# Gate and up projection of a decoder layer: eight k tiles instead of four in one Strassen group, in pieces of 2048 columns

## The chip, the cores and the metric

The kernel runs on one core of one Trainium2 chip. Its time is the device time of one execution in microseconds. Engines: PE is the matrix engine (TensorE), DVE VectorE, ACT ScalarE, POOL GpSimd, SP SyncE, which only issues transfers. 128 partitions of on-chip memory (SBUF) hold the operands; matmuls write into PSUM banks of 128x512 fp32.

## The reference

One layer over 256 tokens of width 2048, in fp32. The changed parts:

```python
def rms_norm(x, g):
    return x * rsqrt(mean(x * x, axis=-1) + EPS) * g

x = x + mixer(rms_norm(x, mix_g))        # pooling and gated delta rule, reads h @ w_in first
x = x + cross_attention(rms_norm(x, xa_g), mem)
h = rms_norm(x, ffn_g)
g = causal_conv3(h @ w_gate) ; u = h @ w_up          # 2048 -> 5632 each
x = x + (silu(g) * u) @ w_down                       # 5632 -> 2048
return rms_norm(x, final_norm_g)
```

(The names of the gains are shortened.) Gate, up and down are the larger part of the arithmetic.

## The kernel before

**Arithmetic.** Every fp32 operand is split into a high part (a cast to the matmul's 32-bit format, on ACT) and a low part (operand minus high part, on DVE). A product is three matmuls: high by high, high by low, low by high (in `product`, lines L876 to L878; 128 rows of weights by 512 columns each). The function `parts` splits a piece of weights: L940 on ACT, L941 on DVE, into tiles `wh` and `wl`.

**Gate and up.** The 5632 columns are handled in 11 blocks (`for b in range(NB)`), each of 512 gate and 512 up columns. A token tile is 128 tokens, and there are two; the sum over 2048 runs over 16 tiles of 128 ("k tiles"). Take a 2x2 product: two halves of tokens, two halves of k, and as column halves gate and up. The weights are b11 (gate, first k half), b12 (up, first half), b21 and b22. For a group of four k tiles (`JS = (0,)`) this product is done by Strassen's scheme in Winograd's form: seven products instead of eight, on sums of the weights (t1 = b11+b12, t2 = t1+b22, t3 = b12+b22, later t2+b21, lines L965 to L969 and L1004 on DVE) and sums of the activations (S3, S5, S6, S7, made once, in `hS`). The other twelve k tiles (`JP`) are done plainly, eight products each group of four. A product there is six matmuls. Banks b1, b2, b3, b5, b6, b7 collect the products; q1 (a copy of b1, L977 on ACT), u2, q1 and c22 (L978 to L980) combine them, and L996 to L1007 scale them by the tokens' factor r3 into c11, c12, c21, c22, L1006 (c11) once a block.

**Rest of a block.** c11 to c22 are turned by 16 transposes (L907), convolved, put through Silu and multiplied into `af` (`convolve`). These steps run in the next block as a "job", a generator that `pump` advances after products. Most blocks' `af` are stored to HBM (`aspill`) and loaded again for the down projection (`arow`).

**Loads.** SP issues all weight loads in program order, each waiting for a free buffer: `wr` has 6 of 0.5 MB, `wh` and `wl` 5 each. The order of the instructions on each engine comes from a scheduler that places the program's operations; the lists below print it.

**Down** uses the same `parts` and buffers, pieces of 0.5 MB. At its end come the residual `fin`, its squares, the final norm with its gain (POOL, L1077) and the stores, t = 0 and then t = 1.

**Start.** x comes in transposed (`xraw`), is scaled and split (L104 on ACT, L105 on DVE, into `hT`), and multiplied by small weights `ba` (bank bps) and by w_in (in_k, weights w0 and then wi, columns in stretches of 128 called h here: h0, h1, h2, ...). The squares for the first norm, xss and xsq, run on POOL (L242 to L245); xsum (L280, DVE) sums them, and a chain xsum, rxps, rx, rxpb brings the norm's factor to PE.

Of the kernel before, what the change touches and what calls it, by code (L numbers as in the profile page):

```python
# [41 lines left out]
def hybrid_trunk(ctx, tc, a, out):  # L42
# [154 lines left out]
    with tc.tile_pool(name="dn", bufs=1, reuse_waits="tile") as dn:  # L197
# [71 lines left out]
        def decays():  # L269
# [9 lines left out]
            with tc.issue_after(last_split[0].ins):  # L279
                dve.tensor_reduce(xsum, xss.rearrange("p k t -> p t k"), AX.X, ALU.add)  # L280
# [591 lines left out]
    def product(ps, stat, j, w, first=False, last=False):  # L872
        for i in range(2):
            xh, xl = stat(j, i)
# [3 lines left out]
            m = pe.matmul(ps, xl, wh, start=False, stop=last and i == 1, skip_group_check=True)  # L878
        pump(m)
# [50 lines left out]
    raw = lambda b, j, w: fp.tile([P, 2, 512], F32, name="wr", tag="wr", bufs=6)  # L930

    def load(b, j, w):
        r = raw(b, j, w)
        nc.sync.dma_start(r, a["w_gu"][b, j, :, w])
        return r

    def parts(src):
# [6 lines left out]
    slot = [0]

    def sumtile():
        slot[0] += 1
        return ring[:, slot[0] % 8].rearrange("p (i c) -> p i c", i=2)

    def results():  # L950
        return [fp.tile([P, 512], F32, name=n, tag=n, bufs=1) for n in ("c11", "c12", "c21", "c22", "q1", "u2")]

    job("xr", rows_of_x())
    c11, c12, c21, c22, q1, u2 = results()
    JS, JP = (0,), (1, 2, 3)
    for b in range(NB):
        b1, b3, b5, b6, b7 = (bank(n) for n in ("b1", "b3", "b5", "b6", "b7"))
        t2s, b21s = {}, {}
        for j in JS:
# [6 lines left out]
            product(b5, S5, j, parts(t1), first=f_, last=l_)
            dve.tensor_tensor(t2, t1, b22, ALU.add)
            product(b6, S6, j, parts(t2), first=f_, last=l_)
            dve.tensor_tensor(t3, b12, b22, ALU.add)  # L969
            product(b7, S7, j, parts(t3), first=f_)  # L970
            t2s[j] = t2
            b21s[j] = load(b, j, 3)
# [192 lines left out]
```

## Time and profile before

| | |
|---|---|
| median of 3 runs | 1547.29 us (1545.36 to 1548.23) |
| the profiled execution | 1547.02 us |
| its span, first to last instruction | 1545.2 us |
| busy: PE, DVE, ACT, POOL | 1499.6, 1068.6, 825.7, 205.7 us |
| moved by DMA | 290.83 MB, 188 GB/s in the mean |

A row of a timeline has a start, a duration, the engine, the line of the kernel, the operation with its output and input, and in brackets how long the engine stood idle before it and what released it. An operation's row is longer than the pitch at which a pipelined engine starts the next: rows overlap.

### The profile page before, as it was taken

How to read it: one execution, taken by the hardware profiler on the slowest of the kernel's cores; microseconds unless marked ns; L12 is line 12 of the kernel's file. 1: busy time of each engine (PE TensorE's matmuls, PEld its weight loads, DVE VectorE, ACT ScalarE, POOL GpSimd, SP SyncE). 2: the span in 40 equal slices, each digit the busy share in tenths (PEclk: the TensorE clock that was granted, in tenths of full speed). 3: DMA queues.
4: the chain of work that ended last, by engine and by line, in shares of the span. 5: the costliest groups of instructions: out<-in, count | busy, mean ns of one | idle time of the engine just before them, and what ended most of it. 6: DMA issues, size and time to landing. Idle time of an engine off the chain costs nothing.

```text
span 1545.2 us, 20429 instructions
## 1 busy us (share of the span) xinstructions
PE 1499.6 (97%) x7788; PEld 1271.9 (82%) x7788; DVE 1068.6 (69%) x1400; ACT 825.7 (53%) x1210; POOL 205.7 (13%) x210
## 2 busy tenths in 40 slices
PE   5999999999999999999979999999999999999997
PEld 3788789888888888998868888888888888888885
DVE  7978887676544676666757778877787886555444
ACT  3555766554444554555546666555556665444433
POOL 4342533341100121001220000000000000000002
PEclk9999999999999999999989999999999999999999
DMA  5445443447555555444538666666666678655562
GB/s 197 169 162 175 174 153 134 139 177 266 192 179 192 185 188 187 146 150 158 188 117 259 206 209 193 193 194 211 215 206 204 202 243 316 199 194 191 194 193 77
DMA packets 67378, 290.83 MB, mean 188 GB/s; under 512 B 11344, under 2 KB 11728, under 8 KB 51152
## 3 DMA queue, kind: packets, MB, share of 16 engines
q1 hardware_dynamic: 66992, 289.01, 54.8%
q8 instruction: 61, 1.00, 0.3%
q10 hardware_dynamic: 288, 0.52, 0.1%
q14 instruction: 37, 0.30, 0.1%
HBM read 279.93 MB, written 9.57 MB: 187 GB/s over the span
## 4 chain that ended last, share of the span: by engine, by line
PE 87%; DVE 7%; POOL 2%; DMA 1%; ACT 1%; issue 1%; SPq 1%; DVEq 0%; POOLq 0%; ACTq 0%
PE b L877 10%; PE b L878 10%; PE b L876 10%; PE acc L1041 5%; PE acc L1043 5%; PE acc L1042 5%; PE xq L142 4%; PE xo L142 4%; PE mix L142 4%; PE kk L142 3%; PE pvs L695 2%; PE pvs L694 2%; PE pvs L693 2%; PE xq L143 2%; PE xo L143 2%; PE mix L143 2%
## 5 line engine op out<-in xcount | busy, mean ns | idle before, releaser
L940 ACT CAST wh<-wr 128x1024 fp32r<-128x1024 f32 x165 | 172.6, 1054 | 141.1 <-PE b L878 134.1
L876 PE MATMUL b<-wh,hP 128*128 128x512 f32 x594 | 233.2, 393 | 6.3 <-ACT wh L940 6.3
L941 DVE TENSOR_TENSOR wl<-wr,wh 128x1024 fp32r<-128x1024 f32 x165 | 199.1, 1220 | 51.1 <-ACT wh L940 50.8
L877 PE MATMUL b<-wl,hP 128*128 128x512 f32 x594 | 231.9, 390 | 0.7 <-DVE wl L941 0.7
L878 PE MATMUL b<-wh,hP 128*128 128x512 f32 x594 | 231.7, 390 | 0.0
L941 DVE TENSOR_TENSOR wl<-wd,wh 128x1024 fp32r<-128x1024 f32 x88 | 107.6, 1224 | 103.8 <-ACT wh L940 103.8
L940 ACT CAST wh<-wd 128x1024 fp32r<-128x1024 f32 x88 | 92.6, 1056 | 120.6 <-PE acc L1043 114.3
L876 PEld LDWEIGHTS b<-wh,hP 128*128 128x128 f32 x594 | 111.7, 188 | 29.2 <-ACT wh L940 6.6
L877 PEld LDWEIGHTS b<-wl,hP 128*128 128x128 f32 x594 | 111.8, 188 | 23.8 <-DVE wl L941 1.2
L878 PEld LDWEIGHTS b<-wh,hP 128*128 128x128 f32 x594 | 111.8, 188 | 23.3
L1041 PE MATMUL acc<-wh,aring 128*128 128x512 f32 x320 | 124.5, 389 | 0.0
L1042 PE MATMUL acc<-wl,aring 128*128 128x512 f32 x320 | 124.5, 389 | 0.0
L1043 PE MATMUL acc<-wh,aring 128*128 128x512 f32 x320 | 124.5, 389 | 0.0
L101 DVE TENSOR_TENSOR wil<-wi,wih 128x1024 fp32r<-128x1024 f32 x78 | 100.5, 1293 | 11.9 <-ACT wih L100 11.5
L1077 POOL TENSOR_TENSOR fin<-fin 128x512 f32<-128x512 f32 x6 | 7.7, 1284 | 720.0 <-ACT fj L1075 719.8
L100 ACT CAST wih<-wi 128x1024 fp32r<-128x1024 f32 x78 | 81.4, 1049 | 8.0 <-DMA wi<-in_w_in 3.3
L142 PE MATMUL xq<-h2T,wqh 128*128 128x512 f32 x240 | 84.9, 393 | 0.0
L142 PE MATMUL kk<-mT,wkh 128*128 128x512 f32 x240 | 84.4, 393 | 0.0
L142 PE MATMUL xo<-oT,woh 128*128 128x512 f32 x240 | 84.3, 392 | 0.0
L142 PE MATMUL mix<-yT,wmh 128*128 128x512 f32 x240 | 84.1, 392 | 0.0
L101 DVE TENSOR_TENSOR wvl<-wv,wvh 128x1024 fp32r<-128x1024 f32 x32 | 39.7, 1240 | 45.3 <-ACT wvh L100 45.3
L1042 PEld LDWEIGHTS acc<-wl,aring 128*128 128x128 f32 x320 | 60.1, 188 | 12.6
(466 smaller groups left out, 3634.3 us busy)
## 6 DMA issues: line engine op xcount, KB each, us to landing
wr<-in_w_gu SPq DMA_DIRECT2D x176, 512.0 KB, 5.0
wd<-in_w_down SPq DMA_DIRECT2D x88, 512.0 KB, 4.7
wi<-in_w_in SPq DMA_DIRECT2D x39, 1024.0 KB, 4.9
wk<-in_w_k SPq DMA_DIRECT2D x16, 1024.0 KB, 4.9
wv<-in_w_v SPq DMA_DIRECT2D x16, 1024.0 KB, 4.9
wm<-in_w_mix SPq DMA_DIRECT2D x16, 1024.0 KB, 4.9
wq<-in_w_xq SPq DMA_DIRECT2D x16, 1024.0 KB, 4.9
wo<-in_w_xo SPq DMA_DIRECT2D x16, 1024.0 KB, 4.9
```

The costliest lines, as they stand in the source:

```text
L100: act.copy(hi, src)
L101: return dve.tensor_tensor(lo, src, hi.bitcast(F32), ALU.subtract)
L142: pe.matmul(ps, h, full, start=kk == 0, stop=False)
L143: i = pe.matmul(ps[:, T:], l, xt[:, 0, :], start=False, stop=False)
L876: pe.matmul(ps, xh, wh, start=first and i == 0, stop=False, skip_group_check=True)
L877: pe.matmul(ps, xh, wl, start=False, stop=False, skip_group_check=True)
L878: m = pe.matmul(ps, xl, wh, start=False, stop=last and i == 1, skip_group_check=True)
L940: act.copy(h, src)
L941: dve.tensor_tensor(l, src, h.bitcast(F32), ALU.subtract)
L1041: pe.matmul(acc[t, n], ah, wh, start=first, stop=False)
L1042: pe.matmul(acc[t, n], ah, wl, start=False, stop=False)
L1043: return pe.matmul(acc[t, n], al, wh, start=False, stop=last)
```

## The change

The k tiles fall into two groups of eight, q = 0 in the Strassen form and q = 1 plain. A product is twelve matmuls, a piece of weights 128x2048 (1 MB). `wr` has 4 buffers, `wh` and `wl` 3 each. b11 is loaded into `tt`, a part of `ring` (two halves, by b % 2), and grows there: b11, plus b12, plus b22, plus b21. The first and third of these sums are transfers from HBM that add to what lies in SBUF, issued by POOL (`join`); the second, and b12 + b22 (in place), are DVE's. So b12 and b21 are read twice. c11 to c22 and `af` move into other parts of `ring`. In the host's layout the weights are cut accordingly.

At the start the squares of x move from POOL to ACT (four of 128x1024), and xsum reduces all 16 tiles at once. In down the pieces are 1 MB, `fin` is loaded late among the weights, and at the end the gain is multiplied on DVE, t = 0's scaling falls into t = 1's sums, and the four stores are 512 KB.

```diff
-            xc = xraw[c // 2][:, (c % 2) * 4:(c % 2) * 4 + 4]
-            if c == 0:
-                pool.tensor_tensor(xss, xc, xc, ALU.mult)
-            else:
-                pool.tensor_tensor(xsq[:, c * 4:c * 4 + 4], xc, xc, ALU.mult)
-                pool.tensor_tensor(xss, xss, xsq[:, c * 4:c * 4 + 4], ALU.add)
+        for c in range(4):
+            act.activation(xsq[:, c * 4:c * 4 + 4], xraw[c // 2][:, (c % 2) * 4:(c % 2) * 4 + 4], AF.Square)
...
-                dve.tensor_reduce(xsum, xss.rearrange("p k t -> p t k"), AX.X, ALU.add)
+                dve.tensor_reduce(xsum, xsq.rearrange("p k t -> p t k"), AX.X, ALU.add)
...
-    def product(ps, stat, j, w, first=False, last=False):
-        for i in range(2):
+    def product(ps, stat, q, w, first=False, last=False):
+        for i in range(4):
...
+    def join(t, b, w):
+        nc.gpsimd.dma_start(t, a["w_gu"][b, 0, :, w], accum_op=ALU.add)
+
+    results = lambda: [ring[:, 4 + n // 2, (n % 2) * 512:(n % 2 + 1) * 512] for n in range(4)]
...
-        for j in JS:
-            f_, l_ = j == JS[0], j == JS[-1]
-            b11, b22, b12 = load(b, j, 0), load(b, j, 2), load(b, j, 1)
-            product(b1, A11, j, parts(b11), first=f_)
-            product(b3, S3, j, parts(b22), first=f_)
-            t1, t2, t3 = sumtile(), sumtile(), sumtile()
-            dve.tensor_tensor(t1, b11, b12, ALU.add)
...
+        tt = ring[:, 2 * (b % 2):2 * (b % 2) + 2].rearrange("p j (i c) -> p (j i) c", i=2)
+        nc.sync.dma_start(tt, a["w_gu"][b, 0, :, 0])
+        b22, b12 = load(b, 0, 2), load(b, 0, 1)
+        product(b1, A11, 0, parts(tt), first=True)
+        join(tt, b, 1)
+        product(b3, S3, 0, parts(b22), first=True)
+        dve.tensor_tensor(b12, b12, b22, ALU.add)
+        product(b7, S7, 0, parts(b12), first=True)
...
+        w = parts(load(b, 1, 1))
+        product(b3, A11, 1, w)
+        product(b2, A21, 1, w, first=True)
+        product(b5, S5, 0, parts(tt), first=True, last=True)
+        dve.tensor_tensor(tt, tt, b22, ALU.add)
+        w = parts(load(b, 1, 2))
+        product(b3, A12, 1, w, last=True)
+        product(b2, A22, 1, w, last=True)
+        product(b6, S6, 0, parts(tt), first=True, last=True)
+        join(tt, b, 3)
...
-        for j in JP:
...
+        w = parts(load(b, 1, 0))
+        product(b1, A11, 1, w)
+        product(b7, A21, 1, w)
+        w = parts(load(b, 1, 3))
+        product(b1, A12, 1, w)
+        product(b7, A22, 1, w)
...
+        product(b1, A12, 0, parts(load(b, 0, 3)), last=True)
+        product(b7, A22, 0, parts(tt), last=True)
...
-    fin = big("fin", [P, 3, D], F32)
-    for t in range(2):
-        nc.sync.dma_start(fin[:, t], xspill[t])
-    nc.sync.dma_start(fin[:, 2], a["fin_row"])
...
+            if m == NB - 2:
+                fin = big("fin", [P, 3, D], F32)
+                for t in range(2):
+                    nc.sync.dma_start(fin[:, t], xspill[t])
+                nc.sync.dma_start(fin[:, 2], a["fin_row"])
+        w = rows(k, 0, 4)
...
-            if n < 3:
-                pool.tensor_tensor(fin[:, t, c], fin[:, t, c], fin[:, 2, c], ALU.mult)
...
+            if (t, n) != (1, 3):
+                with tc.issue_after(i.ins):
+                    dve.tensor_tensor(fin[:, t, c], fin[:, t, c], fin[:, 2, c], ALU.mult)
```

In the changed kernel the split's lines are L938 (ACT) and L939 (DVE), the sums L957 (b12) and L966 (tt), the joins L943, u2, q1 and c22 L974 to L976, the scaling of c11 L990, the squares L249 and xsum L275.

SP's queue from the last xo weights into gate/up, before:

```order
L109 DMA wo<-in_w_xo 128x2048 x16
L934 DMA wr<-in_w_gu 128x1024 x7
L893 DMA xspill<-xt 128x512
L934 DMA wr<-in_w_gu 128x1024 x3
L893 DMA xspill<-xt 128x512
L934 DMA wr<-in_w_gu 128x1024
```
After the loads of w_xo came those of `wr`, with the stores of x between them. The same place now (`ring` is tt):

```order
L109 DMA wo<-in_w_xo 128x2048 x16
L952 DMA ring<-in_w_gu 128x2048 x2
L933 DMA wr<-in_w_gu 128x2048 x3
L891 DMA xspill<-xt 128x512
L933 DMA wr<-in_w_gu 128x2048
L891 DMA xspill<-xt 128x512
```
The loads of the first two blocks' tt stand ahead of all pieces, and the pieces are twice as wide.

DVE in a steady block, around the sums u2, q1 and c22 (names `u_`, `q_`, `c_` and `b_` with a number are u2, q1, c22 and banks), before:

```order
L941 TENSOR_TENSOR wl<-wr,wh 128x1024 x2
L914 SCALAR_TENSOR_TENSOR sg<-gt,prm,sg 128x255
L1004 TENSOR_TENSOR ring<-ring,wr 128x1024
L914 SCALAR_TENSOR_TENSOR sg<-gt,prm,sg 128x254
L978 TENSOR_TENSOR u_9243<-b_9156,q_9242 128x512
L914 SCALAR_TENSOR_TENSOR sg<-gt,prm,sg 128x255
L979 TENSOR_TENSOR q_9242<-b_9155,u_9243 128x512
L914 SCALAR_TENSOR_TENSOR sg<-gt,prm,sg 128x254
L941 TENSOR_TENSOR wl<-wr,wh 128x1024
L925 TENSOR_TENSOR af<-ut,sg 128x512
L941 TENSOR_TENSOR wl<-wr,wh 128x1024 x2
L980 TENSOR_TENSOR c_9241<-q_9242,b_9157 128x512
```
The row of c22, L980, stands behind splits of 1024 columns and small rows. The same place now, where L976 writes c22 (`ring`):

```order
L939 TENSOR_TENSOR wl<-wr,wh 128x2048
L912 SCALAR_TENSOR_TENSOR sg<-gt,prm,sg 128x254
L923 TENSOR_TENSOR ring<-ut,sg 128x512
L939 TENSOR_TENSOR wl<-wr,wh 128x2048
L974 TENSOR_TENSOR u_8202<-b_8010,q_8201 128x512
L939 TENSOR_TENSOR wl<-wr,wh 128x2048
L975 TENSOR_TENSOR q_8201<-b_8009,u_8202 128x512
L957 TENSOR_TENSOR wr<-wr 128x2048
L976 TENSOR_TENSOR ring<-q_8201,b_8011 128x512
L939 TENSOR_TENSOR wl<-ring,wh 128x2048
L986 SCALAR_TENSOR_TENSOR ring<-b_8008,r3r,q_8201 128x512
L987 SCALAR_TENSOR_TENSOR ring<-b_8086,r3r,ring 128x512
```
L976 has moved behind the wide sum L957, which belongs to the next block's b12, and two splits of 2048 columns.

ACT at the start (w0h is the high part of w0, `w_79`), before:

```order
L104 ACTIVATE hT<-xraw,prm 128x256
L100 CAST bah<-ba 128x256
L104 ACTIVATE hT<-xraw,prm 128x256 x7
L100 CAST w0h<-w_79 128x1024
L104 ACTIVATE hT<-xraw,prm 128x256 x8
L100 CAST w0h<-w_79 128x1024
L311 CAST mgr<-cst 128x128
L271 COPY bc<-bps 16x256
L100 CAST wih<-wi 128x1024 x4
```
The two casts of w0 follow the eight L104 that each needs. The same place now:

```order
L104 ACTIVATE hT<-xraw,prm 128x256
L100 CAST bah<-ba 128x256
L104 ACTIVATE hT<-xraw,prm 128x256 x3
L249 ACTIVATE xsq<-xraw 128x1024
L104 ACTIVATE hT<-xraw,prm 128x256 x4
L100 CAST w0h<-w_79 128x1024
L104 ACTIVATE hT<-xraw,prm 128x256 x8
L100 CAST w0h<-w_79 128x1024
L249 ACTIVATE xsq<-xraw 128x1024 x3
L266 COPY bc<-bps 16x256
L306 CAST mgr<-cst 128x128
L100 CAST wih<-wi 128x1024 x4
```
One square has come ahead of the first cast of w0, and three behind the second.

## Rows read from the trace of the kernel before

**Rows 1.** Page, busy us (share of the span) xinstructions.
```profile
PE 1499.6 (97%) x7788; PEld 1271.9 (82%) x7788; DVE 1068.6 (69%) x1400; ACT 825.7 (53%) x1210; POOL 205.7 (13%) x210
```

**Rows 2.** PE's waits: engine line, releaser: us in total, times, longest.
```profile
PE bps L231 <- DVE hT L105: 8.5, 6, 1.7
PE b L876 <- ACT wh L940: 7.5, 3, 6.3
...
PE gps L315 <- DVE gg L308: 1.7, 1, 1.7
```

**Rows 3.** Windows: us, busy (x) of PE PEld DVE ACT POOL, PEclk, DMA share, GB/s.
```profile
930.00:1272.00 342.00, 342.00 (x1575) 284.61 (x1574) 276.43 (x310) 202.89 (x239) 0.00 (x0) 1.00 0.64 206
1272.00:1300.00 28.00, 28.00 (x129) 23.26 (x129) 18.34 (x19) 16.05 (x18) 0.00 (x0) 1.00 0.93 366
```

**Rows 4.** Line L1006: count, duration (ns min/median/max), first and last start.
```profile
L1006 ACT ACTIVATE c<-b,r3r x11: 690/692/692, 852.7 to 1292.2; 128x512 f32<-128x512 f32 x11
```

**Rows 5.** Timeline of PE in gate/up: start, us, engine line op.
```profile
969.18 0.39 PE L878 MATMUL b<-wh,hP 128*128 128x512 f32 x1
...
971.90 0.39 PE L878 MATMUL b<-wh,hP 128*128 128x512 f32 x1
```

**Rows 6.** Groups by form, 895 to 1274: xcount | busy us, mean ns.
```profile
L941 DVE TENSOR_TENSOR wl<-wr,wh 128x1024 fp32r<-128x1024 f32 x130 | 156.9, 1220 | 33.9 <-ACT wh L940 33.7
L940 ACT CAST wh<-wr 128x1024 fp32r<-128x1024 f32 x130 | 136.2, 1055 | 113.0 <-PE b L878 108.9 <-DMA wr<-in_w_gu 2.5 <-DVE c L1000 1.7
...
L978 DVE TENSOR_TENSOR u<-b,q 128x512 f32<-128x512 f32 x9 | 6.1, 681 | 0.0
```

**Rows 7.** Timelines of DVE, POOL and SP at the start.
```profile
8.02 12.83 DVE L105 SCALAR_TENSOR_TENSOR hT<-xraw,prm,hT 128x256 fp32r<-128x256 f32 x6 [0.63 <-ACT hT L104]
20.77 3.37 DVE L101 TENSOR_TENSOR w0l<-w,w0h 128x1024 fp32r<-128x1024 f32 x1
24.06 3.24 DVE L105 SCALAR_TENSOR_TENSOR hT<-xraw,prm,hT 128x256 fp32r<-128x256 f32 x8
...
35.62 2.00 DVE L280 TENSOR_REDUCE xsum<-xss 128x256 f32<-128x1024 f32 x1
...
18.04 5.01 POOL L245 TENSOR_TENSOR xss<-xss,xsq 128x1024 f32<-128x1024 f32 x2
...
20.91 19.34 SPq L109 DMA_DIRECT2D wi<-in_w_in  x5
```

**Rows 8.** Page, DMA issues: xcount, KB each, us to landing.
```profile
wi<-in_w_in SPq DMA_DIRECT2D x39, 1024.0 KB, 4.9
...
fin<-in_fin_row SPq DMA_DIRECT2D x1, 1024.0 KB, 10.3
```

**Rows 9.** Timeline of PE, starts of h1 and h3 of in_k.
```profile
34.59 0.40 PE L142 MATMUL in_k<-hT,wih 128*128 128x512 f32 x1
...
47.48 0.39 PE L142 MATMUL in_k<-hT,wih 128*128 128x512 f32 x1
```

**Rows 10.** Timelines of PE, ACT and SP at the entry of gate/up.
```profile
794.57 0.39 PE L140 MATMUL xo<-oT,woh 128*128 128x512 f32 x1
801.22 0.79 PE L876 MATMUL b<-wh,hP 128*128 128x512 f32 x1 [6.26 <-ACT wh L940]
...
800.13 1.99 ACT L940 CAST wh<-wr 128x1024 fp32r<-128x1024 f32 x2
...
769.99 35.30 SPq L934 DMA_DIRECT2D wr<-in_w_gu  x7
```

**Rows 11.** Timelines of DVE, POOL and SP at the end.
```profile
1532.43 1.82 DVE L1082 SCALAR_TENSOR_TENSOR fin<-fin,fs 128x512 f32<-128x512 f32 x1 [0.67 <-POOL fs L1080]
...
1539.37 0.75 DVE L1082 SCALAR_TENSOR_TENSOR fin<-fin,fs 128x512 f32<-128x512 f32 x1 [1.48 <-POOL fs L1080]
...
1536.34 2.49 POOL L1077 TENSOR_TENSOR fin<-fin 128x512 f32<-128x512 f32 x2 [2.64 <-ACT fj L1075]
...
1540.85 0.33 SPq L1089 DMA_DIRECT2D out_dram<-fin  x1
```

More of the change, by code (lines that the diff above doesn't have):

```diff
@@ L877, in product @@
             pe.matmul(ps, xh, wl, start=False, stop=False, skip_group_check=True)
-            m = pe.matmul(ps, xl, wh, start=False, stop=last and i == 1, skip_group_check=True)
-        pump(m)
+            m = pe.matmul(ps, xl, wh, start=False, stop=last and i == 3, skip_group_check=True)
+            if i % 2:
+                pump(m)
     head_b = NB - 3
@@ L944, in hybrid_trunk, with wide, load, parts @@
[L944 to L951, printed above, removed]
+    def wide(tag, dt=F32, bufs=3):
+        return fp.tile([P, 4, 512], dt, name=tag, tag=tag, bufs=bufs)
+    def load(b, q, w):
+        r = wide("wr", bufs=4)
+        nc.sync.dma_start(r, a["w_gu"][b, q, :, w])
+        return r
+    def parts(src, n=4):
+        h, l = wide("wh", F32R), wide("wl", F32R)
+        act.copy(h[:, :n], src[:, :n])
+        dve.tensor_tensor(l[:, :n], src[:, :n], h.bitcast(F32)[:, :n], ALU.subtract)
+        return h, l
@@ L953, in hybrid_trunk @@
+    def join(t, b, w):
+        nc.gpsimd.dma_start(t, a["w_gu"][b, 0, :, w], accum_op=ALU.add)
+    results = lambda: [ring[:, 4 + n // 2, (n % 2) * 512:(n % 2 + 1) * 512] for n in range(4)]
+    extra = lambda: [fp.tile([P, 512], F32, name=n, tag=n, bufs=1) for n in ("q1", "u2")]
     job("xr", rows_of_x())
-    c11, c12, c21, c22, q1, u2 = results()
-    JS, JP = (0,), (1, 2, 3)
     for b in range(NB):
         b1, b3, b5, b6, b7 = (bank(n) for n in ("b1", "b3", "b5", "b6", "b7"))
-        t2s, b21s = {}, {}
-        for j in JS:
-            f_, l_ = j == JS[0], j == JS[-1]
-            b11, b22, b12 = load(b, j, 0), load(b, j, 2), load(b, j, 1)
-            product(b1, A11, j, parts(b11), first=f_)
-            product(b3, S3, j, parts(b22), first=f_)
-            t1, t2, t3 = sumtile(), sumtile(), sumtile()
-            dve.tensor_tensor(t1, b11, b12, ALU.add)
[L966 to L972, printed above, removed]
@@ L1036, in both, with down @@
         acts[b] = s
-    def down(k, t, n, w, first, last):
+    def down(k, t, n, w, slot, first, last):
         ah, al = (acts[k // 4][:, k % 4, s, half(t)] for s in range(2))
-        wh, wl = (x[:, n % 2] for x in w)
+        wh, wl = w[0][:, slot], w[1][:, slot]
         pe.matmul(acc[t, n], ah, wh, start=first, stop=False)
@@ L1043, in down, with rows @@
         return pe.matmul(acc[t, n], al, wh, start=False, stop=last)
-    def rows(k, c):
-        rw = fp.tile([P, 2, 512], F32, name="wd", tag="wr", bufs=6)
-        nc.sync.dma_start(rw, a["w_down"][k, :, c])
-        return parts(rw)
+    def rows(k, s, n):
+        rw = wide("wr", bufs=4)
+        nc.sync.dma_start(rw[:, :n], a["w_down"][k, :, s:s + n])
+        return parts(rw, n)
     both(1)
-    steps = [(k, c) for c in range(2) for k in order[:4]] + [(k, c) for k in order[4:-2] for c in range(2)]
-    for m, (k, c) in enumerate(steps):
-        if m == 4:
+    for c in range(2):
+        if c:
             drain("cv")
@@ L1056, in hybrid_trunk, with scaled @@
             accs(3)
-        n = blocks.index(k // 4)
-        if k % 4 == 2 and c == 0 and 0 < n < NB - 1:
-            both(n + 1)
-        w = rows(k, c)
+        for k in order[:4]:
+            w = rows(k, 2 * c, 2)
+            for t in range(2):
+                for n in range(2):
+                    i = down(k, t, 2 * c + n, w, n, k == order[0], False)
+                pump(i)
+    for k in order[4:-2]:
+        m = blocks.index(k // 4)
+        if k % 4 == 2 and m < NB - 1:
+            both(m + 1)
+            if m == NB - 2:
+                fin = big("fin", [P, 3, D], F32)
+                for t in range(2):
+                    nc.sync.dma_start(fin[:, t], xspill[t])
+                nc.sync.dma_start(fin[:, 2], a["fin_row"])
+        w = rows(k, 0, 4)
         for t in range(2):
-            for n in (2 * c, 2 * c + 1):
-                i = down(k, t, n, w, k == order[0], False)
-            pump(i)
-    late = [(k, [rows(k, c) for c in range(2)]) for k in order[-2:]]
+            for n in range(4):
+                down(k, t, n, w, n, False, False)
+    late = [(k, rows(k, 0, 4)) for k in order[-2:]]
     fs = xp_.tile([P, 64], F32, name="fs")
     ssq, msf, rf = fs[:, 0:8].rearrange("p (t n) -> p t n", t=2), fs[:, 8:10], fs[:, 10:12]
+    def scaled(t, c, eng):
+        if eng is act:
+            act.activation(fin[:, t, c], fin[:, t, c], AF.Copy, scale=rf[:, t:t + 1])
+        else:
+            dve.tensor_scalar(fin[:, t, c], fin[:, t, c], rf[:, t:t + 1], None, ALU.mult)
+    col = lambda n, m=1: slice(n * 512, (n + m) * 512)
     for t in range(2):
```

76 lines of the change are left out of this document (25 added, 51 removed).

## The prediction

> **What bounds the kernel now.** The page's busy times come first: PE is busy 1499.6 of 1545.2 us [rows 1], so time can go only with matmuls, or where PE waits. The list of PE's waits shows two places that the change touches: the first 57 us (bps on hT 8.5 us, gps on gg 1.7) and the entry of gate/up (one wait of 6.3 us on the cast wh) [rows 2]. The table by windows says what limits gate/up: from 930 to 1272 us PE is busy 342.00 of 342.00 us at granted clock 1.00, DVE 276.43, ACT 202.89, DMA share 0.64 at 206 GB/s [rows 3]. So a block costs what its matmuls cost. The scaling at L1006 comes once a block: eleven from 852.7 to 1292.2 are 43.95 us apart [rows 4]. Matmuls start 0.2267 us apart (twelve from 969.18 to 971.90) [rows 5]; a block's 186 are 42.16 us, and its 16 transposes the other 1.78.
>
> All sums go against the profiled execution, 1547.02 us (span 1545.2 and 1.8 around it), 0.27 below the median of the runs, 1547.29.
>
> **Gate/up, steady blocks.** Seven products of 12 matmuls and eight of 12 replace seven of 6 and 24 of 6: 180 for 186. 6 x 11 x 0.2267 = 15.0 us less, and 42.58 us a block, if PE still never waits. Whether it waits is a matter of four queues.
>
> ACT: a cast of 1024 columns takes 1.055 us [rows 6]; of 2048 twice that at most, and I take 2.0. Eleven a block are 22 us for 19 x 1.055 = 20.0. Slack.
>
> DVE: 1024 columns take 1.220 and 512 take 0.681 [rows 6], so 2048 take 1.220 + 2 x 0.539 = 2.30. Eleven splits and two sums are 29.9 us for 23 x 1.22 = 28.1; with the small forms some 38 of 42.6 us, an average that hides the order. With three wh/wl pairs where there were five, each cast waits for the last product of the piece three earlier. The tightest place is the first b7 product of the plain half, which needs L976 to have read b7. From the end of b6's product DVE has there, by the order, two splits, u2, q1, the wide sum L957 (whose b12 must have landed) and L976: 3 x 2.30 + 3 x 0.68 = 8.9 us; some 0.5 goes for the overlap of neighbouring rows (each starts about 0.09 before the last one's end) and up to 0.3 more because the first split starts early: 8.1 to 8.4. PE's three products on b1 in between last 3 x 2.72 = 8.16. So 0 to 0.3 us of stall; two more places (the split of the next block's tt, c21 before the transposes) have some 0.2 us to spare. I take 0.2 a block, +2.5 in all; bounds 0 and 0.6 a block, +7.
>
> Accumulating transfers (two a block, issued by POOL, 1 MB read from HBM and added to tt in SBUF): the trace has no transfer from POOL into SBUF and none that adds. The nearest rows are a plain load of 1 MB, 4.9 us, and the longest of that size, 10.3 [rows 8]. The first can start when tt is split, about at the block's start; the S5 product comes after five products and the transposes, 15.4 us later, and cast and split want 4.3 of these: 11 us. The second has some 15. Any price up to 11 us is free, and I take 8 to 10, a load's traffic twice.
>
> The Trainium skill (DMA: Bandwidth & Descriptors, Bandwidth) gives 6.15 us for a plain 1 MB load issued from GpSimd, and says under Rules for kernel authors that an accumulate reads its destination and writes it later. If the reading costs as much again, 12.3 us is an estimate from that page; the first transfer is then 1.3 us late in each block and the kernel stands 14 us higher, at 1541. No run here shows it; the trace's plain loads take 4.9.
>
> DMA as a whole: 10 MB a block for 8, and 0.5 of spill, 10.5/42.6 = 246 GB/s; 366 GB/s were moved with PE busy 28.00 of 28.00 [rows 3]. Nothing.
>
> **Start.** While POOL squares (till 23.0 us), six L105 on DVE take 12.83 us and a split 3.37; then eight take 3.24 [rows 7] and a split 1.22 [rows 6]. PE waits for those hT. With the squares on ACT (four of about 1.05, one ahead of the first w0h cast, three behind the second) I walk the queues: the first w0h cast ends at 12.5, its split at 13.7, the second ones at 16.8 and 18.0; PE, slow at first as before, ends its first h at 24.1 instead of 34.59 [rows 9], 10.5 earlier.
> Not all of it lasts. The square behind the second w0h cast frees xraw's first half at about 18 (the first wi was issued at 20.91 [rows 7]); wi lands at 23, is cast by 24, and h1 runs from 24.5 to 30.1. Then DVE has the reduce xsum, now over 128x4096 elements, ahead of the split that h2 needs. 128x1024 took 2.00 us [rows 7]: four times that is 8.0; at the rate of DVE's wide forms (1.05 ns a column) 2.0 + 3.2 = 5.2; I don't see it under 4.4. I take 5.2. The reduce starts at 27.1, the split behind it ends at 28.3 + 5.2 = 33.5, h2 ends some 5.3 later, and h3 begins at 38.8 instead of 47.48: -8.7 (-6 to -9.6). Further on gps may wait a us longer than its 1.7. PE's order up to gate/up is otherwise the same, so the shift carries: -7.5, bounds -3 and -9.5.
>
> **Entry of gate/up.** Before, the loads stood issued from 769.99, and the first cast came at 800.13, when ACT was through with hP and hS; PE's last xo matmul is at 794.57, the first product at 801.22 [rows 10]. Now tt lies in the ring, whose memory oT holds until that last matmul, and both tt loads stand first on SP. Issued at 795.0, landed at 799.9, cast at 802.1, split at 804.4: wh comes 0.9 us later than before, wl 1.7. b22, b12 and w11 stand behind and land about 2.5 us apart, at 805, 808 and 810; products go at the loads' rate until b5. I find the steady rhythm 2 us later than before: +2, bounds 0 and +6.
>
> **Down.** The same matmuls; pieces twice as large, one per 24 x 0.2267 = 5.44 us of PE, four deep. fin's 3 MB now come among the wd loads: 3 x 4.9 us of transfer against pieces in stock for some 16 us. Zero; +3 if the stock runs out.
>
> **Tail.** Before, the last power waits for POOL, which multiplies till 1538.8, and DVE's late sums wait for an L1082 of 1.82 us beside POOL (0.75 alone); the last store is issued at 1540.85 [rows 11], 4.35 before the end. With the multiplies on DVE I walk from the last matmul (1534.9): sum 0.7, square and its sum 0.9, small ones and the power 1.1, scaling 1.2, store 4.7: 8.6 instead of 10.3, -1.8 (-1 to -2.3).
>
> **Sum.** -15.0 + 2.5 - 7.5 + 2 + 0 - 1.8 = -19.8: 1547.0 - 19.8 = 1527.2, so 1527. With all terms at their better ends -15 - 9.5 - 2.3 gives 1520, at their worse ends -15 + 7 - 3 + 6 + 3 - 1 gives 1544, hardly together.
>
> **Rivals.**
> The joins come late (slower than before). If an accumulating transfer takes more than 11 us from issue to landing, the S5 product waits in each of 11 blocks and the excess is paid 11 times. For: it reads what it adds to, goes through another engine's queue, and runs beside 246 GB/s. Against: 10.3 us is the longest 1 MB row, and that one was issued behind two others. It eats all 19.8 us from 12.8; at 14 us the kernel stands at 1527 + 33 = 1560.
> DVE sets the pace. If L976's chain is 1.1 us longer than I walked it (a late b12, or wide forms at twice the narrow price, 2.44, which alone adds 0.4), 12 us of the 15 come back: 1539. For: DVE's 38 of 42.6 us, and three buffers for five. Against: from 512 to 1024 columns the price per column fell.
> The start gives little. If the reduce takes 8 and another small chain on DVE takes what is left, as gps's wait shows can be, 1527 + 6 = 1533.
>
> **Chances.** Forecast 0.56 (its own range 1521 to 1533), little at the start 0.13, DVE's pace 0.17 (1533 to 1543), joins late 0.14 (1540 to 1580). The range with 8 in 10 leaves out most of the joins: 1519 to 1544. Within 0.2% (3.1 us) of before is what a measurement of this kernel can't tell from no change: 0.04, the joins at 12.6 to 13.1 us and the worst of DVE's pace. Slower 0.11, faster 0.85.
>
> **What would show it.** The scaling of c11 (L990) 42.6 to 42.8 us apart, and PE's waits in that stretch on casts, splits or L976 and under 0.5 us each; the transfers from POOL under 11 us, and no S5 product waiting. L105 below 0.5 us throughout the start, h3 at about 39. First product at 802 to 805. From the last matmul to the end 8.6 us. The forecast is wrong if the L990 rows are over 43.3 apart, if xsum takes over 7 us, or if the shift at the start is gone by the time of the xo products.

## The result: slower by 1.4%, and the profile after

| | before | after |
|---|---|---|
| median (runs) | 1547.19 us (4) | 1568.66 us (4), 1566.55 to 1571.08 |
| ratio, 95% interval | | 1.0139 [1.0126, 1.0152] |
| profiled execution, span | 1547.02, 1545.2 us | 1568.48, 1566.5 us |

The forecast was 1527 (1519 to 1544), with 0.85 on faster. It was wrong, and the profile says where. The table splits the two spans at four events that both traces have: the last xo matmul, the first product of gate/up, the scaling of c11 (once a block), and the first matmul of down.

| stretch | before | after | measured | forecast |
|---|---|---|---|---|
| start to last xo matmul | 794.57 | 793.07 | -1.5 | -7.5 |
| last xo matmul to first product | 6.65 | 7.50 | +0.85 | these two: |
| first product to first c11 | 51.44 | 58.43 | +7.0 | +0.9 |
| ten blocks, c11 to c11 | 439.5 | 452.3 | +12.8 | -11.4 |
| last c11 to first down matmul | 1.15 | 2.5 | +1.35 | 0 |
| down | 241.1 | 241.5 | +0.4 | 0 |
| last matmul to the end | 10.7 | 11.2 | +0.5 | -1.8 |
| sum | | | +21.3 | -19.8 |

(Forecast by stretch: of eleven blocks at -1.36 + 0.23 = -1.14, one goes with the entry's +2. The +1.35 behind the last c11 is a shift between rows: the last product on b7 stands behind c11 and has twelve matmuls now for six, 6 x 0.2267 = 1.36 us, which the first block's row no longer holds.)

The lines of the changed kernel that answer to [rows 2 to 4]: PE's waits, then the window of steady blocks, then the scaling of c11, which is L990 now.

```profile
PE gt L905 <- DVE sg L912: 16.2, 10, 2.7
PE b L873 <- ACT wh L938: 9.4, 2, 7.1
...
PE b L874 <- DVE wl L939: 6.3, 3, 3.1
...
PE rxps L165 <- DVE xsum L275: 2.3, 1, 2.3
PE gps L310 <- DVE gg L303: 2.0, 1, 2.0
...
PE b L873 <- DVE ring L976: 1.8, 2, 1.2
```

```profile
930.00:1272.00 342.00, 328.36 (x1475) 268.20 (x1475) 284.07 (x221) 203.80 (x167) 13.03 (x15) 0.99 0.76 238
```

```profile
L990 ACT ACTIVATE ring<-b,r3r x11: 662/669/690, 859.0 to 1311.3; 128x512 f32<-128x512 f32 x11
```

The first row is new: ten times, about once a block, PE stands before L905, the transposes of c11 to c22, waiting for `sg`. That row names no product. PE, which never waited between 930 and 1272 us, is now busy 328.36 of 342 us, and blocks are 45.23 us apart instead of 43.95 (forecast 42.6 to 42.8).

**What a stall looks like.** One stall, in the timelines of POOL, ACT, DVE and PE of the changed kernel (start, us, engine line op, and in brackets the idle time before and its releaser):

```profile
951.39 0.86 POOL L943 DMA_DIRECT2D ring<-in_w_gu  x1 [22.33 <-DVE wl L939]
...
959.45 1.91 ACT L938 CAST wh<-ring 128x2048 fp32r<-128x2048 f32 x1 [2.29 <-DMA ring<-in_w_gu]
961.26 0.56 ACT L910 ACTIVATE sg<-gt,prm 128x256 f32<-128x256 f32 x1
...
961.39 2.29 DVE L939 TENSOR_TENSOR wl<-ring,wh 128x2048 fp32r<-128x2048 f32 x1 [1.92 <-ACT wh L938]
963.60 0.48 DVE L912 SCALAR_TENSOR_TENSOR sg<-gt,prm,sg 128x255 f32<-128x255 f32 x1
963.99 2.28 DVE L966 TENSOR_TENSOR ring<-ring,wr 128x2048 f32<-128x2048 f32 x1
966.19 0.48 DVE L912 SCALAR_TENSOR_TENSOR sg<-gt,prm,sg 128x254 f32<-128x254 f32 x1
...
954.12 0.60 PE L905 MATMUL gt<-cst,ring 128*128 128x128 f32 x4
...
966.82 0.63 PE L905 MATMUL gt<-cst,ring 128*128 128x128 f32 x4 [1.45 <-DVE sg L912]
```

Read it from the bottom. PE waits 1.45 us for the second L912 of a half of `gt`, a bank that the next transposes overwrite. Between the two L912 DVE does a wide sum (2.28 us), and before the first a wide split. Both belong to tt. The L910 on ACT that both L912 need starts at 961.26, directly behind a cast, and that cast is the one that waited 2.29 us for the join. The transposes that filled this `gt` began at 954.12 and took 0.60 us, so the L910 had its input for 6 us and stood only behind the cast. PE doesn't need the cast's result yet, but the cast holds what stands behind it in ACT's queue.

The joins themselves, by the row of their line (the count in the second row is of ACT's waits on them):

```profile
L943 POOL DMA_DIRECT2D ring<-in_w_gu x22: 856/865/1056, 803.5 to 1290.9; - x22
...
  ACT wh L938: 22.4, 9
...
DMA to landing us min/median/max: 7.9/8.5/11.2
```

So the joins cost what the prediction took (8 to 10 us; 8.5 in the median), and no S5 product waits in the steady blocks.

### The profile page after: what moved, and what is told of

Same layout as the page of the kernel before. It is cut to its first block, busy times and chain, and to the rows that moved or that the text cites. A ratio compares the mean times of both kernels' runs of the same rounds, so it can differ in the third digit from the quotient of the medians.

```text
span 1566.5 us, 19587 instructions
## 1 busy us (share of the span) xinstructions
PE 1500.6 (96%) x7722; PEld 1266.5 (81%) x7722; DVE 1086.4 (69%) x1257; ACT 836.0 (53%) x1087; POOL 205.9 (13%) x219
## 4 chain that ended last, share of the span: by engine, by line
PE 60%; issue 22%; DVE 8%; DMA 4%; ACT 3%; POOL 2%; SPq 1%; POOLq 0%; DVEq 0%; ACTq 0%
PE acc L1021 5%; PE acc L1023 5%; PE acc L1022 5%; PE xq L142 4%; PE xo L142 4%; PE mix L142 4%; PE kk L142 3%; DVE wl L939 2%; PE pvs L690 2%; PE pvs L689 2%; PE pvs L688 2%; PE xq L143 2%; PE xo L143 2%; PE mix L143 2%; PE b L874 2%
## 5 line engine op out<-in xcount | busy, mean ns | idle before, releaser
L939 DVE TENSOR_TENSOR wl<-wr,wh 128x2048 fp32r<-128x2048 f32 (+1 forms) x125 | 277.3, 2220 | 127.0 <-ACT wh L938 126.1
L938 ACT CAST wh<-wr 128x2048 fp32r<-128x2048 f32 (+1 forms) x125 | 231.8, 1856 | 155.2 <-PE acc L1023 107.4
L873 PE MATMUL b<-wh,hP 128*128 128x512 f32 x484 | 192.2, 398 | 11.1 <-ACT wh L938 9.4
L874 PE MATMUL b<-wl,hP 128*128 128x512 f32 x484 | 190.3, 393 | 4.6 <-DVE wl L939 4.6
L875 PE MATMUL b<-wh,hP 128*128 128x512 f32 x484 | 190.1, 393 | 0.0
L939 DVE TENSOR_TENSOR wl<-ring,wh 128x2048 fp32r<-128x2048 f32 x44 | 100.8, 2292 | 54.5 <-ACT wh L938 54.5
L873 PEld LDWEIGHTS b<-wh,hP 128*128 128x128 f32 x484 | 91.7, 189 | 33.8 <-ACT wh L938 10.0
L938 ACT CAST wh<-ring 128x2048 fp32r<-128x2048 f32 x44 | 83.9, 1907 | 54.0 <-PE b L875 28.3
L874 PEld LDWEIGHTS b<-wl,hP 128*128 128x128 f32 x484 | 91.7, 190 | 23.9 <-DVE wl L939 5.5
L875 PEld LDWEIGHTS b<-wh,hP 128*128 128x128 f32 x484 | 91.7, 189 | 19.3
L943 POOL DMA_DIRECT2D ring<-in_w_gu x22 | 19.3, 878 | 468.3 <-DVE wl L939 319.8
L874 PE MATMUL b<-wl,hS 128*128 128x512 f32 x176 | 70.7, 402 | 1.7 <-DVE wl L939 1.7
L873 PE MATMUL b<-wh,hS 128*128 128x512 f32 x176 | 71.5, 406 | 0.0
```

The source lines that it names most:

```text
L875: m = pe.matmul(ps, xl, wh, start=False, stop=last and i == 3, skip_group_check=True)
L938: act.copy(h[:, :n], src[:, :n])
L939: dve.tensor_tensor(l[:, :n], src[:, :n], h.bitcast(F32)[:, :n], ALU.subtract)
```

## The experiments

Each theory's words stand as they were before the run. "The changed kernel" is the starting point unless it is said otherwise. Ratios are against the kernel before, run on the same chip (its medians there are 1546.9 to 1547.3 us).

**1. The join's landing (a first join of 512 columns instead of 2048; it leaves 1536 of the sum's 2048 columns without b12).**

```diff
-        nc.gpsimd.dma_start(t, a["w_gu"][b, 0, :, w], accum_op=ALU.add)
+        nc.gpsimd.dma_start(t[:, :3 * (w != 1) + 1], a["w_gu"][b, 0, :, w, :3 * (w != 1) + 1], accum_op=ALU.add)
```

> The first accumulating transfer of each block carries 512 of its 2048 columns (three quarters of that sum are left out); the order of the instructions on every engine is as in the changed kernel. Theory (ACT's queue): the cast of tt waits 2.3 us for the transfer (8.1 us from issue to landing) at the head of ACT's queue, and L910 behind it, and by that L912, the release of gt and the next transposes; with a transfer of 3 to 5 us the wait of gt on L912 (16.2 us in ten blocks) goes, blocks 1 to 10 come at 42.9 to 43.3 us instead of 45.2 in the mean, and the time falls by 18 to 22 us to 1547 to 1551. Rival (DVE's wide pieces): L912 waits for the splits and sums of 2.29 us ahead of it on DVE whatever the transfer does; the waits on gt stay within 0.4 us a block, and the time within 4 us.

Measured 1547.00 us, 1.0003 [0.9992, 1.0013]: 21.7 below the changed kernel, with the same order of instructions on every engine. The wait on `sg` is gone, and c11 comes every 43.11 us. The rows are DMA issues, the window and L990 of this run:

```profile
ring<-in_w_gu POOLq DMA_DIRECT2D x11, 1024.0 KB, 8.6
...
ring<-in_w_gu POOLq DMA_DIRECT2D x11, 256.0 KB, 4.2
```

```profile
930.00:1272.00 342.00, 341.44 (x1557) 279.54 (x1556) 300.87 (x232) 215.45 (x177) 13.90 (x16) 1.00 0.71 232
```

```profile
L990 ACT ACTIVATE ring<-b,r3r x11: 668/671/690, 858.3 to 1289.4; 128x512 f32<-128x512 f32 x11
```

The join lands 4 us earlier and the ten blocks are 452.3 - 431.1 = 21.2 us shorter. So the steady loss hangs on when the first join lands. It doesn't yet say whether by its product or by what stands behind its cast; the next run does.

**2. The same cast moved behind the second L910 of `gt`** (`behind` issues after a remembered instruction; the join is whole again).

```diff
-        product(b5, S5, 0, parts(tt), first=True, last=True)
+        product(b5, S5, 0, behind(0, lambda: parts(tt)), first=True, last=True)
```

> The cast of tt for the S5 product is issued behind the second L910 of the block's first half; the transfers stay as they are. Theory (ACT's queue): L910 and L912 no longer wait for the transfer, gt is released some 5 us earlier, and the waits on gt go: blocks 1 to 10 at 42.9 to 43.5 us, time 1548 to 1553. The S5 product, for which cast and split have 4 us after the landing, doesn't wait. Rival (DVE's wide pieces): the L912 wait behind other splits instead, and a block gains under 0.5 us. Rival (the next wait): the product behind L976 waits instead, 1 us a block: time 1556 to 1560.

1557.73 us, 1.0064 [1.0049, 1.0079]: in the range of the second rival, the next wait. The wait on `sg` is gone with only the order changed, and run 1 lost it with DVE's wide pieces in their places, so ACT's queue was its cause. But half of the gain is eaten by a new wait (first fence, PE's waits; second, the timelines of DVE and PE at one of its nine places):

```profile
PE b L873 <- DVE ring L983: 10.4, 9, 2.8
```

```profile
984.05 2.29 DVE L964 TENSOR_TENSOR wr<-wr 128x2048 f32<-128x2048 f32 x1 [0.88 <-DMA wr<-in_w_gu]
986.26 0.68 DVE L983 TENSOR_TENSOR ring<-q,b 128x512 f32<-128x512 f32 x1
...
986.99 0.50 PE L873 MATMUL b<-wh,hP 128*128 128x512 f32 x1 [0.84 <-DVE ring L983]
```

L983 is c22 (L976 of the changed kernel), which must read b7 before the first plain product adds to that bank. In front of it DVE's queue holds the wide sum of the next block's b12, and that one waits for its load. It is the place of the prediction's second rival, with a late b12 as it said, and it is the same pattern again: an instruction that nobody needs yet waits at the head of a queue.

**3. That wide sum moved behind c22 as well.**

```diff
-        dve.tensor_tensor(b12, b12, b22, ALU.add)
+        behind(4, lambda: dve.tensor_tensor(b12, b12, b22, ALU.add))
-        dve.tensor_tensor(c22, q1, b7, ALU.subtract)
+        seen[4] = dve.tensor_tensor(c22, q1, b7, ALU.subtract)
```

> The cast of tt stands behind the second L910 as in the run with the late cast, and the wide sum of the next block's b12 and b22 is issued behind L976 (c22) instead of ahead of it. Theory (an in-order queue again): the 0.9 us a block that the late cast left, on the product behind c22, came of this sum, which waits up to 1.9 us for its b12 to land and takes 2.29; with it behind c22 blocks 1 to 10 come at 43.0 to 43.4 us and the 4 us of block 0's wait for the split of w10 go: time 1542 to 1548. Rival (c22's chain is bound by the splits ahead of it): blocks at 44.0 or more, time within 3 us of 1557.7. Rival: the transposes wait for c21 instead, since the sum now stands ahead of c21 and the splits: 1550 to 1556.

1544.80 us, 0.9987 [0.9977, 0.9996]: as expected. The waits on `sg` and on c22 are gone from the steady blocks, where 1.9 us in ten blocks are left, none over 0.7; c11 comes every 43.17 us, and every 42.9 where no wait falls:

```profile
L997 ACT ACTIVATE ring<-b,r3r x11: 672/687/690, 854.2 to 1285.9; 128x512 f32<-128x512 f32 x11
```

Two moved instructions, none removed: 23.9 us less than the changed kernel, 20.6 of them in the ten blocks.

**4. No joins: both sums by DVE from the loaded pieces** (two wide sums more on DVE, 2 MB less from HBM a block).

```diff
-        join(tt, b, 1)
+        dve.tensor_tensor(tt, tt, b12, ALU.add)
...
-        join(tt, b, 3)
...
-        product(b1, A12, 0, parts(load(b, 0, 3)), last=True)
+        b21 = load(b, 0, 3)
+        product(b1, A12, 0, parts(b21), last=True)
+        dve.tensor_tensor(tt, tt, b21, ALU.add)
```

> Both accumulating transfers are replaced by sums on DVE of pieces that are loaded anyway (tt + b12, tt + b21), so ACT waits for no transfer from POOL and 2 MB a block less are read; DVE gets two more sums of 2.29 us a block. Theory (the transfers hold up ACT's queue, and DVE has little left): the waits of gt on L912 change their releaser from the late cast to wide forms on DVE; DVE's work of about 38 us a block becomes 42.5 of 42.6, so PE waits for DVE at several places, 1.5 to 3 us a block: time 1560 to 1575. Rival (the transfers alone are to blame): blocks at 43.0 to 43.5 us, time 1547 to 1553.

1620.86 us, 1.0476 [1.0460, 1.0491]: both missed, by far. c11 comes every 50.66 us. The window, PE's waits in it, and the timelines of DVE, ACT and PE around one pair of waits:

```profile
930.00:1272.00 342.00, 313.98 (x1342) 251.96 (x1341) 283.24 (x211) 182.69 (x150) 0.00 (x0) 0.95 0.49 177
```

```profile
PE b L873 <- ACT wh L938: 21.1, 12, 1.8
PE b L874 <- DVE wl L939: 6.9, 7, 1.0
```

```profile
1017.84 2.27 DVE L957 TENSOR_TENSOR wr<-wr 128x2048 f32<-128x2048 f32 x1
...
1020.20 1.90 ACT L938 CAST wh<-wr 128x2048 fp32r<-128x2048 f32 x1 [3.67 <-DVE wr L957]
...
1022.15 0.50 PE L873 MATMUL b<-wh,hS 128*128 128x512 f32 x1 [1.78 <-ACT wh L938]
1024.41 0.80 PE L873 MATMUL b<-wh,hP 128*128 128x512 f32 x1 [1.75 <-ACT wh L938]
```

DVE is busy 283 of 342 us, not full, as in the changed kernel. What fails is a chain: sum on DVE, cast on ACT, split on DVE, product, each behind others in its queue. The releasers show it, but the sums weren't tried at other places, so the price holds for this order. Behind the second of the two waits shown the matmul takes 0.80 us where it took 0.50 behind the first, and the granted clock is 0.95 over the window. Against this order the transfers that add were worth far more than they cost; I hadn't considered that.

**5. The old start in the changed kernel** (squares on POOL again, xsum over 4 k tiles).

```diff
-        for c in range(4):
-            act.activation(xsq[:, c * 4:c * 4 + 4], xraw[c // 2][:, (c % 2) * 4:(c % 2) * 4 + 4], AF.Square)
+            if c == 0:
+                pool.tensor_tensor(xss, xc, xc, ALU.mult)
+            else:
+                pool.tensor_tensor(xsq[:, c * 4:c * 4 + 4], xc, xc, ALU.mult)
+                pool.tensor_tensor(xss, xss, xsq[:, c * 4:c * 4 + 4], ALU.add)
```

> The changed kernel with the start of the kernel before: squares on POOL, xsum over four k tiles. Theory (start): in the changed kernel PE has its first h done 10.4 us earlier, but the last xo matmul ends only 1.50 us earlier (793.07 for 794.57), since xsum took 7.40 us and PE waited and went at half clock behind it; so undoing the start costs 1.5 us and no more: 1570, and the last xo matmul is at 794.6 again. Rival: part of the start's gain is hidden in what follows, and undoing it costs 5 us or more. Rival: the new start harms (DVE's reduce), and undoing it gains.

1575.37 us (1569.17 to 1577.60), 1.0173 [1.0149, 1.0198]; in the profiled run, 1569.17, the last xo matmul is at 794.06 for 793.07. The scatter is wide, and the medians are 6.7 apart (as the first rival had it) where the profiled runs are 0.7 apart (as the theory had it): nothing is decided. So the next run tried it in the kernel before.

**6. The new start in the kernel before** (the opposite diff, nothing else).

> The kernel before with the changed start alone (squares on ACT, xsum over 16 k tiles). Theory: the first h ends 10 us earlier, xsum of 7.40 us gives most of it back; the last xo matmul moves by 1.5 to 4 us and the time with it: 1543 to 1546. Rival (the forecast's start term, 7.5 us): 1539 to 1541. Rival (the start gains nothing): 1547 to 1548.

1544.20 us, 0.9978 [0.9968, 0.9987], as expected: the start alone gives 3 us, not 7.5. Its waits are those of the changed kernel there (rxps on xsum 2.3 us, gps 2.0, dps 2.6).

**7. The long reduce replaced: three sums of 128x1024 on DVE ahead of the splits, then a reduce of 128x1024.** First in the changed kernel:

```diff
+        for c in range(1, 4):
+            add = dve.tensor_tensor(xsq[:, 0:4], xsq[:, 0:4], xsq[:, c * 4:c * 4 + 4], ALU.add)
...
+            dve.tensor_reduce(xsum, xsq[:, 0:4].rearrange("p k t -> p t k"), AX.X, ALU.add)
-                dve.tensor_reduce(xsum, xsq.rearrange("p k t -> p t k"), AX.X, ALU.add)
```

> The squares stay on ACT; DVE adds their four parts (three sums of 128x1024, 1.22 us each) as they come and reduces the sum over four k tiles (2.0 us), all before the first split of wi. Theory: PE no longer waits for xsum (2.3 us) nor goes at half clock behind it (7 us of pairs at 0.64 for 0.35 us, 3 us lost); h3 begins at 36 to 37 instead of 42.8. Of these 6 us the chain to gps begins 10 us earlier and gps doesn't wait, which saves 2 us and another stretch at half clock; the last xo matmul moves to 784 to 788, time 1560 to 1564. Rival (the chain of small forms behind xsum on DVE and ACT is the bound from 50 to 80 us whatever PE does): the last xo matmul moves by under 2 us, time 1567 to 1569.

1562.91 us, 1.0103 [1.0086, 1.0119], as expected: 5.8 below the changed kernel, and the last xo matmul is at 787.76 for 793.07. Then the same in the kernel before:

> The kernel before, with the squares on ACT and the sum over k tiles by three DVE sums of 128x1024 (1.2 us each) ahead of the splits of wi, then a reduce of 128x1024 (2.0 us) in place of 128x4096 (7.4). Theory (the long reduce makes PE wait 2.3 us for xsum, and what is lost behind it is TensorE's clock at its lower level): no wait on xsum, and the last xo matmul some 5 to 7 us earlier than before: 1540 to 1542. Rival (later chains on DVE and ACT, gps and dps, take the gain whatever the reduce costs): the same 3 us as with the start alone, 1544.

1541.52 us, 0.9968 [0.9957, 0.9980]; the last xo matmul is at 788.22. This too is as expected. The reduce now takes 1.92, PE no longer waits for xsum, and the granted clock stays at 1.00 where it fell (timeline of DVE, then the windows):

```profile
21.06 1.92 DVE L254 TENSOR_REDUCE xsum<-xsq 128x256 f32<-128x1024 f32 x1
```

```profile
34.00:38.00 4.00, 4.00 (x23) 3.34 (x22) 2.56 (x7) 1.55 (x3) 0.00 (x0) 1.00 0.58 209
38.00:42.00 4.00, 4.00 (x23) 3.35 (x22) 3.65 (x13) 2.86 (x8) 1.51 (x1) 1.00 0.37 115
```

Against the start with the long reduce it is 2.7 us less by medians, and 5.1 by the last xo matmul of the profiles. The two medians are from different chips and their ratios' intervals overlap; in the changed kernel the intervals are apart.

**8. All together.** Cast and wide sum late, the tree, r3 before the first product (`drain("r")` ahead of the blocks), and the stores of x issued by ACT:

```diff
-            nc.sync.dma_start(xspill[t, :, n * 512:(n + 1) * 512], xt)
+            nc.scalar.dma_start(xspill[t, :, n * 512:(n + 1) * 512], xt)
```

> All together: late cast, sum behind c22, xsum by three sums and a reduction over four k tiles before the splits of wi, the factor r3 computed ahead of the first product, the stores of x issued by ACT instead of SP. Theory: steady blocks at 43.0 to 43.4 us (1542 to 1548), 4 to 6 us less from the start as the run with the sums showed, 2 to 4 less in block 0, whose second split waited 1.7 us behind r3 on DVE: time 1534 to 1541, below the kernel before (1547.3). Rival: block 0 is bound by its first four loads, which start only when the last xo matmul frees the ring, and gains nothing from r3 and the stores: 1538 to 1543.

1543.56 us, 0.9981 [0.9971, 0.9990]: missed. The first block gained nothing, 57.0 us from its first product to its c11 for 56.4 in run 3: a copy on ACT waited 4.2 us for a store ahead of a cast. Without these two:

> The changed kernel with the cast of tt behind gt's second half, the wide sum of b12 behind c22, and the tree of sums at the start. Theory (the three losses add): 1544.8 of the kernel without the tree less the 4 to 6 us that the tree gave in the changed kernel: 1539 to 1541, with no steady wait over 0.3 us and block 0 still at 59. Rival (what the start gains, gate/up's entry waits for, because its loads set the pace there): 1544.

1541.16 us (1536.33 to 1545.49), 0.9966 [0.9953, 0.9980], at the upper end of the range and with a wide scatter, though with a shorter first block than I said, 54.3 us to its c11. Then r3 early with the stores on SP, and each next block's tt loaded late, behind the load of w13 (the sixth piece of a block in the edit, not the fifth; 5 is its place in `seen`):

```diff
-        nc.sync.dma_start(tt, a["w_gu"][b, 0, :, 0])
+        behind(5, lambda: nc.sync.dma_start(tt, a["w_gu"][b, 0, :, 0]))
```

> As the kernel with the tree and both moves, and in addition r3 before gate/up's first product and each next block's load of tt behind the fifth piece of the block before (at the entry the second block's 1 MB no longer goes ahead of the first block's pieces). Theory (block 0 is paced by its loads: 1 MB less ahead of b22 is some 3 us): block 0 55 to 57 us and 1536 to 1539. Rival (block 0 is paced by waits of DVE and ACT and by TensorE at its lower level, not by bytes): block 0 stays at 59, 1539 to 1544; or the late load of tt comes too late in the later blocks, waits on the cast wh at each block's start, 1545 and more.

1539.35 us, 0.9952 [0.9940, 0.9964]: in the range of the rival. The first c11 comes 54.5 us behind the first product, as without the two edits, and 62.9 behind the last xo matmul for 61.8. So the two together don't shorten the entry, which speaks against the 1 MB ahead of the pieces as what paced it; they were not tried apart. It is the fastest of all runs, but its interval overlaps the one of the kernel before with the tree alone (0.9957 to 0.9980): that the regrouped gate/up is worth anything by itself is not shown. The profiles of these two (spans 1538.6 and 1538.2) say where its gain goes: the ten blocks take 432.3 us for 439.6, but from the last xo matmul to the first c11 it is 62.9 for 57.4, behind the last c11 1.35 more, and from the last matmul to the end 11.5 for 10.7.

## Why the prediction was wrong

**Gate/up, steady: this step failed.** The 180 matmuls came as said, and the durations too: a cast of 2048 columns 1.91 us (2.0 predicted), a split 2.29 (2.30). What failed is "Slack" for ACT and the check of the join against its own product alone. I allowed the join 11 us because S5 comes that late. It took 8.5. But its cast stands in ACT's queue ahead of the second L910, DVE then puts a split and a sum of 2.3 us each around the two L912, and the transposes in PE wait. I forecast 0.2 us of stall a block, at L976, and that place has 1.8 us in ten blocks, as priced; the wait on `sg`, which my sum held at nothing, has 16.2. Runs 1 and 2 show the cause, one by the landing and one by the order.

How far this explains the miss is read from the windows from the first c11 to the last, of the changed kernel and of run 3:

```profile
859.00:1311.30 452.30, 434.32 (x1961) 354.92 (x1960) 375.90 (x292) 270.74 (x224) 17.35 (x20) 0.99 0.78 242
```

```profile
854.20:1285.90 431.70, 429.77 (x1961) 352.76 (x1960) 374.68 (x292) 270.83 (x224) 17.36 (x20) 1.00 0.81 252
```

Ten blocks of 42.58 without a stall are 425.8 us, and 452.3 were measured. Of the 26.5 between, 18.0 are waits. Another 4.5 went with them: PE is busy 434.3 us for 429.8 in run 3 with the same matmuls, at a granted clock of 0.99 for 1.00. The last 4.0, 0.4 a block, stay in run 3 too. I carried over 1.78 us for everything that isn't a product; I haven't broken down what it is now.

**Rival 1, the joins late,** priced the time (1540 to 1580) and not the reason. Its condition, over 11 us, doesn't hold in the median (the longest of 22 is 11.2), and S5 never waits in the steady blocks. The prediction's estimate of 12.3 us, worked out from the Trainium skill (DMA: Bandwidth & Descriptors, Bandwidth and Rules for kernel authors), is too high; the measurement, 7.9 to 11.2, decides. **Rival 2, DVE's pace,** is what came up in run 2, at L976 and by a late b12, once the first wait was gone.

**The start: this step was mis-sized.** The first h ended early as walked, and L105 is short. But xsum takes 7.40 us and not 5.2; "over 7" was the mark for a wrong forecast. Timelines of DVE and PE, then the windows behind the wait, of the changed kernel:

```profile
25.80 7.40 DVE L275 TENSOR_REDUCE xsum<-xsq 128x256 f32<-128x4096 f32 x1
...
33.35 0.73 PE L165 MATMUL rxps<-cst,xsum 128*128 128x1 f32 x4 [2.28 <-DVE xsum L275]
...
42.84 0.58 PE L142 MATMUL in_k<-hT,wih 128*128 128x512 f32 x1
```

```profile
34.00:38.00 4.00, 3.69 (x13) 3.13 (x13) 3.81 (x5) 0.00 (x0) 1.62 (x1) 0.50 0.32 84
38.00:42.00 4.00, 4.00 (x18) 3.44 (x18) 1.65 (x4) 1.59 (x3) 0.00 (x0) 0.69 1.01 414
```

PE waits 2.28 us, and behind the wait the granted clock is 0.50, the lower level (1.2 GHz), at which a pair of matmuls takes 0.64 us instead of 0.35. So h3 begins at 42.84 for 47.48 [rows 9]: -4.6, not -8.7. The rest is lost at gps (a wait of 1.99 us at 56.87, again at the lower clock till 60.9) and dps. The third rival named both, a longer reduce and what comes behind it, and priced them at 6 us, which leaves the 1.5 that this profile shows. I had counted a wait as its own length and nothing after it. Of 7.5 us 1.5 were left in this profile and 3 by the medians of run 6; with the short reduce 5 to 6 (run 7).

**The entry of gate/up: +2 in the sum, +0.9 over its two rows, +7.8 measured there; this step was mis-sized too.** Counted from the last xo matmul the first product came 0.85 us later, as walked (0.9). What I missed is the block behind it. The timelines of SP, PE and DVE, and SP's waits:

```profile
793.49 0.80 SPq L952 DMA_DIRECT2D ring<-in_w_gu  x2
798.85 1.28 SPq L933 DMA_DIRECT2D wr<-in_w_gu  x3
...
802.90 0.80 PE L874 MATMUL b<-wl,hP 128*128 128x512 f32 x1 [1.53 <-DVE wl L939]
...
811.06 0.50 PE L874 MATMUL b<-wl,hS 128*128 128x512 f32 x1 [1.74 <-DVE wl L939]
818.35 0.52 PE L873 MATMUL b<-wh,hP 128*128 128x512 f32 x1 [2.24 <-ACT wh L938]
850.65 0.50 PE L874 MATMUL b<-wl,hP 128*128 128x512 f32 x1 [3.06 <-DVE wl L939]
...
845.50 2.29 DVE L957 TENSOR_TENSOR wr<-wr 128x2048 f32<-128x2048 f32 x1 [1.91 <-DMA wr<-in_w_gu]
```

```profile
SPq L933 <- DVE hP L101: 4.5, 1, 4.5
```

Not only tt waits for the stage before, as I said; the pieces do too. Their first load waits 4.5 us for DVE's split of hP and is issued at 798.85, where before seven stood issued from 769.99 [rows 10]. Four waits follow, 8.57 us in all, for 2.55 before, and the clock over 801 to 855 is 0.87 (0.94 before). The last one is the wide sum again, waiting for its load ahead of a split. With the second tt loaded late and r3 early (run 8) the entry was as long, so neither is shown to be the cause; placing the pieces in memory that is free earlier wasn't tried, so this stays open: even in the last kernel of run 8 the first block takes 54.5 us to its c11 for 43.2 of a steady one (before 51.4 for 44.0).

**Down** came as forecast (+0.4 for 0). **The tail** gave +0.5 for -1.8. The last sum, the last scaling and the last store, timelines of DVE and ACT:

```profile
1556.86 0.69 DVE L1070 TENSOR_TENSOR fin<-acc,fin 128x512 f32<-128x512 f32 x1
...
1559.64 1.15 ACT L1060 ACTIVATE fin<-fin,fs 128x1024 f32<-128x1024 f32 x1 [1.05 <-POOL fs L1084]
...
1560.82 0.37 ACTq L1089 DMA_DIRECT2D out_dram<-fin  x1
```

The scaling took the 1.2 us that I walked, but that store, 512 KB, takes 5.7 to the end where I walked 4.7 (the last one before took 4.35 [rows 11]). And the last sum, walked right behind the last matmul (which ends at 1555.73), starts 1.1 us later: DVE's multiplies and scalings, 0.69 and 0.48 us, stand between its sums. No run undid this by itself.

## What to carry to other kernels

For each instruction that waits on something new, list what stands behind it in its own engine's queue, and who waits for that, not only who waits for its result: here a transfer that was in time for its product cost PE 16.2 us of waits in ten blocks through a cast that nobody needed yet. Where pieces get wider and buffers fewer, look for such a cast or sum at the head of a queue and issue it behind the small instruction that others need (two moves, 24 us). And a stall of PE of about 2 us is priced at more than its length where the trace shows the granted clock low behind it.

## What the hardware showed that I had not expected

- A transfer from POOL that adds 1 MB from HBM to SBUF lands 8.5 us after its issue in the median (7.9 to 11.2), a plain 1 MB load of the same kernel in 4.9 to 6.5; adding 256 KB takes 4.2. Issuing one occupies POOL for 0.87 us.
- The reduce along a strided axis takes 2.00 us from 128x1024 and 7.40 from 128x4096, 1.8 to 2.0 ns an element of a partition, where DVE's sums of 128x2048 take 1.1 ns.
- After a PE wait of about 2.3 us the lower clock lasted differently long in executions of the same start: in the changed kernel the clock was 0.69 from 38 to 42 us and at 56 to 60 again, in the kernel of run 3 it was back at 38 us:

```profile
34.00:38.00 4.00, 3.77 (x14) 3.29 (x15) 3.65 (x5) 0.00 (x0) 1.62 (x1) 0.57 0.33 98
38.00:42.00 4.00, 4.00 (x23) 3.13 (x22) 2.49 (x9) 2.08 (x5) 0.00 (x0) 1.00 1.01 422
```

The last xo matmul then comes at 790.26 instead of 793.07. A difference of 3 us between two single profiles with such a wait near the start says nothing of an edit elsewhere.
